# Layer 1's first channel-mixer product as seven products of halves for eight, past two blocks

## The chip, the cores and the metric

The kernel runs on one core of one Trainium2 chip. The metric is the device time of one execution in microseconds (us). Before the change it is 1830.53 us, the median of three runs (1828.48 to 1834.18).

## What is computed

Two layers of a diffusion backbone over 512 latent tokens (width 1024) and 256 context tokens. Each layer has a mixer (attention, retention and a state-space part over one input projection) and a channel mixer. In layer 1 the context's output is not needed, so its channel mixer works on 512 tokens alone. Cut to what matters here, all in float32:

```
h2 = rmsnorm(x, norm_g[2]) * (1 + sc2) + sh2            # 512 x 1024
u  = square(relu(h2 @ w_ff1))                           # w_ff1 1024 x 4096
x  = x + g2 * rmsnorm(u @ w_ff2, norm_g[3])             # w_ff2 4096 x 1024
```

## The kernel before, in words

Every float32 operand of a product is split into a rounded high part (ScalarE's copy to the `F32R` type) and a low part (the difference, taken by VectorE). A product is then three matmuls, high by high, high by low and low by high, which accumulate in one bank of PSUM. This is `mm3`, and it is why all matmuls of the profile have the lines L523, L524 and L525.

Weights come from HBM by DMAs on SP's queue, 512 KB at a time, into raw tiles (`wraw`, tag `wr`, three buffers). `wunit` splits them: ScalarE writes `wh` (L277), VectorE writes `wl` (L278). The pool `wp` has three buffers each of `wh` and `wl`, and every one holds 2048 columns, that is two raw tiles.

The channel mixer of layer 1 is `ff_phase(1, ...)`. It goes over eight blocks of 512 hidden columns. In a block:

- The first product, `ff1_part`, makes four banks `f`, each of 128 hidden columns by 512 tokens. A weight slice of 128 x 128 is the stationary operand, the tokens `h_h` and `h_l` move. A bank takes 8 x 3 matmuls of 512 columns, a block 96. For block 0, the four banks are begun earlier, in the output projection's stage, with 256 of the tokens; so its matmuls are 256 columns wide.
- The squared ReLU: ScalarE takes the ReLU out of PSUM (L1503), GpSimd squares (L1504), VectorE casts to `uh` (L1505) and subtracts to `ul` (L1506).
- The second product, `ff2`: for each of the four groups of 128 tokens (`tt`), two banks of 512 output columns in the PSUM tags `pb` and `pc` (two buffers each), 4 x 3 matmuls of 512 columns for each bank, 96 in a block. VectorE adds the banks to `acc` (L1532 copies in block 0, L1534 adds after it).

At the last block `sandwich` follows for each `tt`: the norm of `acc`, the gate, the residual and the store.

PSUM has eight banks: tag `pa` with two buffers of two banks, `pb` and `pc` with two of one bank each. The program's order is a priority: the framework builds each engine's own order when it compiles, from what is ready and which buffers are free, and each engine then runs that order.

## Time and profile before

| what | value |
|---|---|
| median of three runs | 1830.53 us (1828.48 to 1834.18) |
| profiled execution | 1831.16 us, span 1829.4 us |
| mean granted clock of TensorE | 0.979 |
| TensorE (PE) busy | 1737.7 us, 95% of the span |
| weight loads (PEld) busy | 1433.7 us, 78% |
| VectorE (DVE) busy | 1208.8 us, 66% |
| ScalarE (ACT) busy | 701.7 us, 38% |
| GpSimd (POOL) busy | 342.4 us, 19% |

The span runs from the first to the last instruction; the execution's own time is a little longer. A matmul's recorded duration overlaps the next one's, so the cost of one matmul in a stream is the distance from start to start, not its duration. The columns of the views are told beside their first rows below.

### The profile page before, as it was taken

How to read it: one execution, taken by the hardware profiler on the slowest of the kernel's cores; microseconds unless marked ns; L12 is line 12 of the kernel's file. 1: busy time of each engine (PE TensorE's matmuls, PEld its weight loads, DVE VectorE, ACT ScalarE, POOL GpSimd, SP SyncE). 2: the span in 40 equal slices, each digit the busy share in tenths (PEclk: the TensorE clock that was granted, in tenths of full speed). 3: DMA queues.
4: the chain of work that ended last, by engine and by line, in shares of the span. 5: the costliest groups of instructions: out<-in, count | busy, mean ns of one | idle time of the engine just before them, and what ended most of it. 6: DMA issues, size and time to landing. Idle time of an engine off the chain costs nothing. (4 is left out here: it accounts for less than half of the span.)

```text
span 1829.4 us, 24602 instructions
## 1 busy us (share of the span) xinstructions
PE 1737.7 (95%) x8991; PEld 1433.7 (78%) x8991; DVE 1208.8 (66%) x2474; ACT 701.7 (38%) x1270; POOL 342.4 (19%) x376
## 2 busy tenths in 40 slices
PE   7998999998999999999999999999988999999997
PEld 2887978657777888888888878887877788888886
DVE  5788976767567566566566587898877644444445
ACT  5553366743561201211201266545762622222222
POOL 0127222312000100100100111453121111111112
PEclk9999999998999999999999999999987999999999
DMA  8420443476435434444344443233343523333332
GB/s 282 123 61 30 133 123 101 119 204 177 162 120 137 126 105 126 128 113 117 116 116 116 128 150 116 68 106 104 106 121 85 179 67 94 102 94 100 104 95 92
DMA packets 189077, 217.00 MB, mean 119 GB/s; under 512 B 67666, under 2 KB 142236, under 8 KB 188956
## 3 DMA queue, kind: packets, MB, share of 16 engines
q1 hardware_dynamic: 188956, 215.43, 39.7%
q8 instruction: 71, 1.16, 0.3%
q14 instruction: 50, 0.41, 0.1%
HBM read 189.66 MB, written 25.72 MB: 118 GB/s over the span
## 5 line engine op out<-in xcount | busy, mean ns | idle before, releaser
L523 PE MATMUL f<-h_h,wh_f 128*128 128x512 f32 (+1 forms) x800 | 281.2, 352 | 1.4 <-ACT h_h L504 1.4
L524 PE MATMUL f<-h_l,wh_f 128*128 128x512 f32 (+1 forms) x800 | 281.7, 352 | 0.8 <-DVE h_l L505 0.8
L525 PE MATMUL f<-h_h,wl_f 128*128 128x512 f32 (+1 forms) x800 | 282.3, 353 | 0.0
L523 PE MATMUL f<-wh_g,uh 128*128 128x512 f32 x640 | 252.8, 396 | 4.6 <-DVE acc L1532 1.9
L524 PE MATMUL f<-wl_g,uh 128*128 128x512 f32 x640 | 252.5, 394 | 0.0
L525 PE MATMUL f<-wh_g,ul 128*128 128x512 f32 x640 | 251.8, 393 | 0.0
L1504 POOL TENSOR_TENSOR r<-r 128x768 f32<-128x768 f32 (+1 forms) x64 | 94.0, 1469 | 834.2 <-ACT r L1503 823.1
L277 ACT ACTIVATE wh_f<-wr_f 128x1024 fp32r<-128x1024 f32 x64 | 66.4, 1054 | 375.2 <-PE f L525 135.4
L1534 DVE TENSOR_TENSOR acc<-acc,f 128x512 f32<-128x512 f32 x140 | 96.1, 687 | 120.8 <-PE f L525 119.4
L523 PEld LDWEIGHTS f<-h_h,wh_f 128*128 128x128 f32 x800 | 153.2, 192 | 23.4 <-ACT h_h L504 1.5
L524 PEld LDWEIGHTS f<-h_l,wh_f 128*128 128x128 f32 x800 | 152.2, 190 | 23.0 <-DVE h_l L505 1.0
L525 PEld LDWEIGHTS f<-h_h,wl_f 128*128 128x128 f32 x800 | 152.4, 191 | 20.9
L461 DVE SCALAR_TENSOR_TENSOR ga<-wr_mg,cg_a,ga 128x512 f32<-128x512 f32 x216 | 153.7, 764 | 15.2 <-DMA wr_mg<-in_w_mod_dram 15.1
L523 PEld LDWEIGHTS f<-wh_g,uh 128*128 128x128 f32 x640 | 120.1, 188 | 33.9 <-DVE acc L1532 2.3
L525 PEld LDWEIGHTS f<-wh_g,ul 128*128 128x128 f32 x640 | 120.2, 188 | 28.6
L524 PEld LDWEIGHTS f<-wl_g,uh 128*128 128x128 f32 x640 | 120.3, 188 | 27.3
L1503 ACT ACTIVATE r<-f 128x768 f32<-128x768 f32 (+1 forms) x64 | 44.7, 698 | 192.2 <-PE f L525 128.2
L1505 DVE CAST uh<-r 128x768 fp32r<-128x768 f32 (+1 forms) x64 | 32.3, 505 | 123.7 <-POOL r L1504 123.7
L278 DVE TENSOR_TENSOR wl_g<-wr_g,wh_g 128x1024 fp32r<-128x1024 f32 x62 | 76.7, 1242 | 53.8 <-ACT wh_g L277 53.8
L278 DVE TENSOR_TENSOR wl_f<-wr_f,wh_f 128x1024 fp32r<-128x1024 f32 x64 | 77.7, 1221 | 50.1 <-ACT wh_f L277 50.1
L277 ACT ACTIVATE wh_g<-wr_g 128x1024 fp32r<-128x1024 f32 x64 | 67.3, 1056 | 96.6 <-DMA wr_g<-in_w_ff_dram 55.2
L523 PE MATMUL xbc<-h_h,wh_xbc 128*128 128x512 f32 (+1 forms) x208 | 71.9, 345 | 1.9 <-ACT cin L785 1.9
(403 smaller groups left out, 3711.0 us busy)
## 6 DMA issues: line engine op xcount, KB each, us to landing
wr_f<-in_w_ff_dram SPq DMA_DIRECT2D x64, 512.0 KB, 3.8
wr_g<-in_w_ff_dram SPq DMA_DIRECT2D x64, 512.0 KB, 3.6
wr_mg<-in_w_mod_dram SPq DMA_DIRECT2D x192, 128.0 KB, 2.9
wr_m<-in_w_mod_dram SPq DMA_DIRECT2D x24, 512.0 KB, 4.0
m<-in_w_mod_dram SPq DMA_DIRECT2D x32, 256.0 KB, 5.1
wr_o<-in_w_out_dram SPq DMA_DIRECT2D x16, 512.0 KB, 4.2
wr_xbc<-in_w_in_dram SPq DMA_DIRECT2D x14, 512.0 KB, 5.4
xmid<-xt SPq DMA_DIRECT2D x10, 512.0 KB
```

Of the source, the lines that this page charges most:

```text
L277: S.activation(hv[:, a0 : a0 + an], r, AF.Copy)
L278: (lo_eng or V).tensor_tensor(lv[:, a0 : a0 + an], r, hv[:, a0 : a0 + an].bitcast(F32), ALU.subtract)
L461: V.scalar_tensor_tensor(acc[:, s], r2[:, k % 2], w, acc[:, s], ALU.mult, ALU.add)
L523: T.matmul(o, a[0], b[0], start=first, stop=False)
L524: T.matmul(o, a[0], b[1], start=False, stop=False)
L525: return T.matmul(o, a[1], b[0], start=False, stop=last)
L1503: S.activation(r, q[:, :NT], AF.Relu)
L1504: G.tensor_tensor(r, r, r, ALU.mult)
L1505: V.tensor_copy(uh, r)
L1534: V.tensor_tensor(acc[tt][:, ns], acc[tt][:, ns], qs[tt][half], ALU.add)
```

## The change

From its third block on (3072 of 4096 hidden columns), the first product of layer 1's channel mixer is made by one level of Strassen's form. Tokens, inner dimension and hidden columns are each cut into two halves, and seven products of halves stand for eight; the combinations of halves are formed by additions. `ff_phase` gives way for layer 1 to a new function, `ff_seven`:

- Blocks 0 and 1 stay plain. Their squares move from GpSimd to ScalarE, and so does the cast to the high part.
- Six units `u` take the place of blocks 2 to 7. A unit has 256 hidden columns of the one half and 256 of the other. It loads four raw quarter tiles (512 KB each), GpSimd forms four sums of them (`weight_sum`), and `weight_part` splits seven operands. Each product has 2 x 4 x 3 matmuls of 256 columns.
- Once, GpSimd adds up the four quarters of the tokens and forms four differences (`tw`, `tx`); `token_part` splits them.
- Products are gathered outside PSUM: three sums in SBUF (`sums`), then four results `x` by VectorE; ReLU, square and cast by ScalarE.
- The second product keeps its matmuls, in two parts for each group of tokens (`s...0` and `s...1`). Its first weights lie in a buffer of their own.
- All steps are units with names, and a list (`PLAN[2]`) gives their order. `sandwich` takes its tiles from the tag `rw`.

The diff, cut:

```diff
+    RW=6,
+    UB=2,
+    XQ=2,
...
+    2: """
+        a010 a001 lw10 l200 a000 l201 tw12 a011 a100 wr012 s000 s001 s020 s021 wr022 lw11 s030 s031 s010 a110
+        s011 wr011 tw11 tw22 tx11 tx12 tx22 wr021 wp00 tw21 ws01 l210 ws03 a101 ws02 wr111 wp01 a111 p00 wr112
+        s110 wp02 tx21 l211 s111 tp1 s120 s100 wp03 s101 tp4 p01 tp2 wp04 s130 wp05 s121 tp3 p02 q00 q01 wr122
...
+        wr522 s501 q40 s521 q41 s530 ws44 wp46 q42 wr512 l261 q43 s511 s531 p50 ws51 s600 wp51 p51 ws52 wp52
+        s630 p52 wp54 s631 s620 s621 ws53 l270 wp53 s610 s601 q50 wp55 s611 q52 l271 q51 ws54 wp56 q53 s700
+        s701 s710 s711 s720 s721 s730 s731
+    """.split(),
...
-    def sandwich(pool, o, gate, xsrc, xdst, tt, nl, nwhich, hT, eng, bufs=2, half_bank=None, geng=None):
-
-        xt = pool.tile([128, D], F32, tag="xt", name="xt", bufs=bufs)
-        t = pool.tile([128, D], F32, tag="tt", name="tt", bufs=bufs)
+    def sandwich(pool, o, gate, xsrc, xdst, tt, nl, nwhich, hT, eng, bufs=2, half_bank=None, geng=None, tags=("xt", "tt")):
+
+        xt = pool.tile([128, D], F32, tag=tags[0], name="xt", bufs=bufs)
+        t = pool.tile([128, D], F32, tag=tags[1], name="tt", bufs=bufs)
...
+    def ff_seven(l, fp, h2T, pre):
+        NQ = 4
+        NS = 2
+        HID = (FF - NS * 512) // 2
+        acc = [fp.tile([128, D], F32, tag="acc", name=f"acc{l}{t}", bufs=NQ) for t in range(NQ)]
+        NB = FF // 512
+        w1, qpre = pre
+        hh, hl = h2T
+        rw = lambda name: fp.tile([128, 1024], F32, tag="rw", name=f"{name}{l}", bufs=KNOBS["RW"])
+        q4 = lambda ap: ap.rearrange("p (t k c) -> p t k c", t=2, k=4)
+        k4 = lambda ap: ap.rearrange("p (k c) -> p k c", k=4)
+        UNITS, AFTER = {}, {}
+        def unit(name, f, *after):
+            UNITS[name] = f
+            AFTER[name] = [n for n in after if n]
+        part = lambda ap, j, t: ap[:, 2 * t : 2 * t + 2, 4 * j : 4 * j + 4, :]
+        B = {"11": (0, 0), "12": (0, 1), "21": (1, 0), "22": (1, 1)}
+        side = {n: (part(hh, *B[n]), part(hl, *B[n])) for n in B}
+        full = {}
+        def whole(n):
+            b = q4(rw(f"b{n}"))
+            G.tensor_tensor(b, side[n][0].bitcast(F32), side[n][1].bitcast(F32), ALU.add)
+            full[n] = b
+        def token_part(n, b):
+            b = full[b]
+            dst = side["12"] if n == "t4" else tuple(q4(fp.tile([128, 1024], F32R, tag=f"{n}{i}", name=f"{n}{i}{l}")) for i in "hl")
+            S.activation(dst[0], b, AF.Copy)
+            V.tensor_tensor(dst[1], b, dst[0].bitcast(F32), ALU.subtract)
+            side[n] = dst
+        def sub(o, a, b):
+            G.tensor_tensor(full[o], full[a], full[b], ALU.subtract)
+        std = [f"a{NS - 1}{v}{fc}" for v in range(2) for fc in range(2)]
+        for n in ("12", "11", "22", "21"):
+            unit(f"tw{n}", lambda n=n: whole(n), "a000")
+        unit("tx11", lambda: sub("11", "12", "11"), "tw11", "tw12")
+        unit("tx12", lambda: sub("12", "22", "12"), "tw22", "tx11")
+        unit("tx22", lambda: sub("22", "22", "11"), "tx12")
+        unit("tx21", lambda: sub("21", "21", "22"), "tw21", "tx22")
+        unit("tp2", lambda: token_part("t2", "22"), "tx22")
+        unit("tp1", lambda: token_part("t1", "11"), "tx22")
+        unit("tp3", lambda: token_part("t3", "12"), "tx12")
+        unit("tp4", lambda: token_part("t4", "21"), "tx21", "tw12", *std)
+        raw, op, slot = {}, {}, {}
+        def weight_load(u, n):
+            i, j = int(n[0]) - 1, int(n[1]) - 1
+            raw[u, n] = k4(rw(f"w{n}_{u}"))
+            nc.sync.dma_start(raw[u, n], krows(w_ff1[l], 4 * j, 4, 512 * NS + 256 * u + HID * i, 256))
+        def weight_sum(u, o, a, b, how):
+            if (u, o) not in raw:
+                raw[u, o] = k4(rw(f"{o}_{u}"))
+            G.tensor_tensor(raw[u, o], raw[u, a], raw[u, b], how)
+        def weight_part(u, i, n):
+            if i % 2 == 0:
+                h, lo = (wp.tile([128, 2144], F32R, tag=t, name=f"{t}_s{l}{u}{i}", bufs=3) for t in ("wh", "wl"))
+                slot[u, i], slot[u, i + 1] = ((k4(h[:, o : o + 1024]), k4(lo[:, o : o + 1024])) for o in (0, 1024))
+            h, lo = slot[u, i]
+            S.activation(h, raw[u, n], AF.Copy)
+            V.tensor_tensor(lo, raw[u, n], h.bitcast(F32), ALU.subtract)
+            op[u, i] = h, lo
+        def product(q, a, n):
+            for c in range(2):
+                fs = slice(c * 128, (c + 1) * 128)
+                qv = q[:, c].rearrange("p (t c) -> p t c", c=128)
+                for k in range(4):
+                    mm3(qv, (a[0][:, k, fs], a[1][:, k, fs]), (side[n][0][:, :, k, :], side[n][1][:, :, k, :]),
+                        k == 0, k == 3)
+        def hidden(U, half, x):
+            ts = slice(256 * half, 256 * half + 256)
+            S.activation(x, x, AF.Square)
+            S.activation(U[0][:, :, ts], x, AF.Copy)
+            V.tensor_tensor(U[1][:, :, ts], x, U[0][:, :, ts].bitcast(F32), ALU.subtract)
+        Us = {}
+        def new_u(b, s):
+            if (b, s) not in Us:
+                Us[b, s] = tuple(fp.tile([128, 2, 512], F32R, tag=f"u{i}", name=f"u{i}{l}{b}{s}", bufs=KNOBS["UB"]) for i in "hl")
+            return Us[b, s]
+        xq = lambda name: fp.tile([128, 2, 256], F32, tag="xq", name=f"{name}{l}", bufs=KNOBS["XQ"])
+        pq = lambda name, i: fp.tile([128, 2, 256], F32, tag=f"pq{i}", name=f"{name}{l}")
+        ps, sums = {}, {}
+        def first(u, i):
+            if i == 0:
+                ps[u] = pA([128, 2, 2, 256], f"s0{l}{u}")
+                sums[u] = [pq(f"p{j}_{u}", j) for j in range(3)]
+                p1, u1, u4 = sums[u]
+                product(ps[u][:, 0], op[u, 0], "11")
+                S.activation(p1, ps[u][:, 0], AF.Copy)
+            elif i == 1:
+                p1, u1, u4 = sums[u]
+                product(ps[u][:, 1], op[u, 1], "t1")
+                V.tensor_tensor(u4, p1, ps[u][:, 1], ALU.add)
+            else:
+                p1, u1, u4 = sums[u]
+                A = pA([128, 2, 2, 256], f"s1{l}{u}")
+                product(A[:, 0], op[u, 2], "t2")
+                V.tensor_tensor(u1, p1, A[:, 0], ALU.add)
+                V.tensor_tensor(u4, u4, A[:, 0], ALU.add)
+        LATE = (("t3", 1, 1, 2, 3), ("t4", 1, 0, 1, 4), ("21", 0, 0, 0, 5), ("22", 0, 1, 2, 6))
+        def rest(u, i):
+            n, s, half, a, o = LATE[i]
+            q = (pB, pC)[i % 2]([128, 2, 256], f"s{i + 2}{l}{u}")
+            product(q, op[u, o], n)
+            if i == 0:
+                V.tensor_tensor(sums[u][1], sums[u][1], q, ALU.add)
+            x = xq(f"c{i}_{u}")
+            V.tensor_tensor(x, sums[u][a], q, ALU.add)
+            S.activation(x, x, AF.Relu)
+            hidden(new_u(u + NS, s), half, x)
+        def plain(b, v, fc):
+            w = w1[v] if b == 0 else wst[b, v]
+            q = qpre[2 * v + fc] if b == 0 else pA([128, TOK], f"f1{l}{b}{v}{fc}")
+            ff1_part(q, h2T, w, fc, 256 if b == 0 else 0, 512)
+            x = xq(f"r{b}{v}{fc}").rearrange("p a c -> p (a c)")
+            S.activation(x, q[:, 0:512], AF.Relu)
+            S.activation(x, x, AF.Square)
+            U = new_u(b, v)
+            S.activation(U[0][:, fc], x, AF.Copy)
+            V.tensor_tensor(U[1][:, fc], x, U[0][:, fc].bitcast(F32), ALU.subtract)
+        wst, w2, qs, gates = {}, {}, {}, []
...
+        def w2_load(b, v):
+            r0 = 4 * NS + 2 * (b - NS)
+            r = (4 * b + 2 * v) if b < NS else r0 + v * (HID // 128)
+            w2[b, v] = wunit(wcols(w_ff2[l], r, [(0, 0, 1024)]), (128, 2, 1024), f"g{l}{b}{v}", None, fp if v == 0 else None)
+        def second(b, tt, s):
+            cols = slice(tt * 128, (tt + 1) * 128)
+            if s == 0:
+                qs[b, tt] = [P([128, 512], f"f2{l}{b}{tt}{half}") for half, P in enumerate((pB, pC))]
+            U = Us[b, s]
+            for half in range(2):
+                ns = slice(half * 512, (half + 1) * 512)
+                q = qs[b, tt][half]
+                for i in range(2):
+                    mm3(q, (U[0][:, i, cols], U[1][:, i, cols]), (w2[b, s][0][:, i, ns], w2[b, s][1][:, i, ns]),
+                        s + i == 0, s + i == 2)
+                if s == 0:
+                    continue
+                if b == 0:
+                    V.tensor_copy(acc[tt][:, ns], q)
+                else:
+                    V.tensor_tensor(acc[tt][:, ns], acc[tt][:, ns], q, ALU.add)
+            if s and b == NB - 1:
+                if not gates:
+                    gates.append(gate_row(fp, l, 1, 0))
+                sandwich(fp, (acc[tt][:, 0:512], acc[tt][:, 512:1024]), gates[0], rows(xmid[l], tt), rows(out[0], tt),
+                         tt, l + 1, 0, None, G if tt < NQ - 1 else V, 6, None, G if tt < NQ - 1 else V, ("rw", "rw"))
...
+        for b in range(NB):
+            for v in range(2):
+                unit(f"l2{b}{v}", lambda b=b, v=v: w2_load(b, v))
+            u = b - NS
+            if u >= 0:
+                for n in ("11", "21", "22", "12"):
+                    unit(f"wr{u}{n}", lambda u=u, n=n: weight_load(u, n))
+                unit(f"ws{u}1", lambda u=u: weight_sum(u, "s1", "21", "22", ALU.add), f"wr{u}21", f"wr{u}22")
+                unit(f"ws{u}2", lambda u=u: weight_sum(u, "s2", "s1", "11", ALU.subtract), f"ws{u}1", f"wr{u}11")
+                unit(f"ws{u}3", lambda u=u: weight_sum(u, "21", "11", "21", ALU.subtract), f"ws{u}1")
+                unit(f"ws{u}4", lambda u=u: weight_sum(u, "12", "12", "s2", ALU.subtract), f"ws{u}2", f"wr{u}12", f"wp{u}5")
+                for i, (n, a) in enumerate((("11", "wr{}11"), ("s1", "ws{}1"), ("s2", "ws{}2"), ("21", "ws{}3"), ("22", "wr{}22"),
+                                            ("12", "wr{}12"), ("12", "ws{}4"))):
+                    unit(f"wp{u}{i}", lambda u=u, i=i, n=n: weight_part(u, i, n), a.format(u), f"wp{u}{i - 1}" if i % 2 else None)
+                for i, t in enumerate((None, "tp1", "tp2")):
+                    unit(f"p{u}{i}", lambda u=u, i=i: first(u, i), f"wp{u}{i}", t, f"p{u}{i - 1}" if i else None)
+                for i, t in enumerate(("tp3", "tp4", None, None)):
+                    unit(f"q{u}{i}", lambda u=u, i=i: rest(u, i), f"wp{u}{i + 3}", t, f"p{u}2", f"q{u}0" if i else None)
+            for tt in range(NQ):
+                for v in range(2):
+                    made = [f"a{b}{v}{fc}" for fc in range(2)] if u < 0 else [f"q{u}{i}" for i in ((2, 3), (0, 1))[v]]
+                    unit(f"s{b}{tt}{v}", lambda b=b, tt=tt, v=v: second(b, tt, v), f"l2{b}{v}", *made, f"s{b}{tt}0" if v else None,
+                         f"s{b - 1}{tt}1" if b else None)
...
-        ff_phase(1, fp, h2T, pre, None)
+        ff_seven(1, fp, h2T, pre)
```

## Rows read from the trace of the kernel before

**Rows 1.** Busy time by engine in a stretch: start:end, length, busy, counts, clock, DMA.

```profile
core 0: us, PE busy (x) PEld busy (x) DVE busy (x) ACT busy (x) POOL busy (x), PEclk, DMA share, GB/s
...
1486.00:1819.60 333.60, 333.60 (x1437) 270.06 (x1436) 146.58 (x193) 76.75 (x100) 49.66 (x35) 1.00 0.29 94
```

**Rows 2.** Timeline of PE, first product, 512 columns: start, duration, instruction.

```profile
1552.05 0.39 PE L523 MATMUL f<-h_h,wh_f 128*128 128x512 f32 x1
...
1570.07 0.39 PE L523 MATMUL f<-h_h,wh_f 128*128 128x512 f32 x1
```

**Rows 3.** Timeline of PE, second product, and its last matmul.

```profile
1803.87 0.40 PE L523 MATMUL f<-wh_g,uh 128*128 128x512 f32 x1
...
1819.27 0.40 PE L523 MATMUL f<-wh_g,uh 128*128 128x512 f32 x1
...
1819.73 0.40 PE L525 MATMUL f<-wh_g,ul 128*128 128x512 f32 x1
```

**Rows 4.** Timeline where block 0 ends: 256-column matmuls behind the first 512-column ones.

```profile
1480.10 0.39 PE L523 MATMUL f<-wh_g,uh 128*128 128x512 f32 x1
...
1481.41 1.25 DVE L1505 CAST uh<-r 128x512 fp32r<-128x512 f32 x1 [0.93 <-POOL r L1504]
...
1482.72 0.50 PE L523 MATMUL f<-wh_g,uh 128*128 128x512 f32 x1 [1.76 <-DVE uh L1505]
...
1483.29 0.28 PE L523 MATMUL f<-h_h,wh_f 128*128 128x256 f32 x1
...
1483.41 0.19 PEld L525 LDWEIGHTS f<-h_h,wl_f 128*128 128x128 f32 x1
...
1485.78 0.29 PE L523 MATMUL f<-h_h,wh_f 128*128 128x256 f32 x1
```

**Rows 5.** Groups of instructions, 1486.0 to 1819.6 us: count, busy us, mean ns, idle before.

```profile
L1504 POOL TENSOR_TENSOR r<-r 128x512 f32<-128x512 f32 x29 | 41.1, 1416 | 276.1 <-ACT r L1503 276.1
L1534 DVE TENSOR_TENSOR acc<-acc,f 128x512 f32<-128x512 f32 x54 | 37.1, 688 | 67.8 <-PE f L525 67.6
L278 DVE TENSOR_TENSOR wl_g<-wr_g,wh_g 128x1024 fp32r<-128x1024 f32 x28 | 34.2, 1223 | 34.0 <-ACT wh_g L277 34.0
L277 ACT ACTIVATE wh_g<-wr_g 128x1024 fp32r<-128x1024 f32 x28 | 29.5, 1055 | 53.6 <-PE f L524 32.8 <-DMA wr_g<-in_w_ff_dram 20.8
L1506 DVE TENSOR_TENSOR ul<-r,uh 128x512 fp32r<-128x512 f32 x29 | 20.0, 689 | 0.5
L1503 ACT ACTIVATE r<-f 128x512 f32<-128x512 f32 x29 | 17.1, 588 | 28.7 <-issue 23.5 <-PE f L525 5.1
L1505 DVE CAST uh<-r 128x512 fp32r<-128x512 f32 x29 | 12.4, 427 | 39.3 <-POOL r L1504 39.3
```

**Rows 6.** GpSimd's 128x1024 subtraction of weights: min/median/max ns, first and last start.

```profile
L278 POOL TENSOR_TENSOR wl_g<-wr_g,wh_g x2: 2394/2400/2407, 1454.2 to 1456.6; 128x1024 fp32r<-128x1024 f32 x2
```

**Rows 7.** Timelines of DVE and POOL where their instructions overlap, and one alone.

```profile
1564.20 1.22 DVE L278 TENSOR_TENSOR wl_g<-wr_g,wh_g 128x1024 fp32r<-128x1024 f32 x1 [3.02 <-ACT wh_g L277]
...
1564.73 1.59 POOL L1504 TENSOR_TENSOR r<-r 128x512 f32<-128x512 f32 x1 [4.73 <-ACT r L1503]
1569.61 1.04 POOL L1504 TENSOR_TENSOR r<-r 128x512 f32<-128x512 f32 x1 [3.29 <-ACT r L1503]
...
1815.04 3.52 POOL L1437 TENSOR_TENSOR tt<-acc,gr 128x512 f32<-128x512 f32 x2 [2.33 <-DVE acc L1534]
...
1817.60 0.97 DVE L1438 TENSOR_TENSOR oss<-oss 128x1 f32<-128x1 f32 x1 [0.85 <-ACT junk L1435]
...
1823.70 0.16 DVE L1438 TENSOR_TENSOR oss<-oss 128x1 f32<-128x1 f32 x1
```

**Rows 8.** The chain that ended last, from PE's end on: start, us, what.

```profile
1822.25 0.61 DVE acc L1534
...
1824.87 0.75 DVE xt L1441
1825.62 0.66 DVEq L1676
```

More of the change, by code (lines that the diff above doesn't have):

```diff
@@ L115 @@
         wo8
+    """.split(),
[3 more added lines that the diff above has]
+        s110 wp02 tx21 l211 s111 tp1 s120 s100 wp03 s101 tp4 p01 tp2 wp04 s130 wp05 s121 tp3 p02 q00 q01 wr122
+        wp10 s131 q02 wr121 ws11 ws04 wp06 p10 q03 wp11 ws13 p11 ws12 l220 wp12 wr221 l221 wp13 p12 s210 s200
+        s230 s231 wr222 wr211 s201 s220 wp14 s221 q10 ws21 wr212 wp15 ws14 ws22 wp20 q12 wp16 s211 ws23 wr322
+        wp22 q13 l230 q11 wp21 p20 s300 s310 p21 l231 p22 wp23 s320 wp24 wp25 s301 ws24 q20 wp26 s330 q23
+        wr311 s321 wr321 s311 wp30 q22 s331 ws31 ws32 p30 q21 l240 wp32 s400 wp31 ws33 p31 wp34 s410 wr312 p32
+        wr412 s430 wp33 l241 s401 s411 q30 wr411 s420 wr422 wp35 q32 q31 ws34 s431 s421 wp36 wr421 wp40 p40
+        l250 l260 ws41 wp41 wr511 l251 ws42 q33 s510 s500 wp42 p41 ws43 wp43 s520 wp44 wp45 wp50 wr521 p42
+        wr522 s501 q40 s521 q41 s530 ws44 wp46 q42 wr512 l261 q43 s511 s531 p50 ws51 s600 wp51 p51 ws52 wp52
+        s630 p52 wp54 s631 s620 s621 ws53 l270 wp53 s610 s601 q50 wp55 s611 q52 l271 q51 ws54 wp56 q53 s700
+        s701 s710 s711 s720 s721 s730 s731
     """.split(),
@@ L1551, in ff_phase, with w1_load @@
         return (hTn, kvw) if wc else None
+    def ff_seven(l, fp, h2T, pre):
[116 more added lines that the diff above has]
+        wst, w2, qs, gates = {}, {}, {}, []
+        def w1_load(b, v):
+            wst[b, v] = load_w1(l, b, v)
+        def w2_load(b, v):
[24 more added lines that the diff above has]
+                         tt, l + 1, 0, None, G if tt < NQ - 1 else V, 6, None, G if tt < NQ - 1 else V, ("rw", "rw"))
+        for b in range(NS):
+            for v in range(2):
+                if b:
+                    unit(f"lw{b}{v}", lambda b=b, v=v: w1_load(b, v))
+                for fc in range(2):
+                    unit(f"a{b}{v}{fc}", lambda b=b, v=v, fc=fc: plain(b, v, fc), f"lw{b}{v}" if b else None)
+        for b in range(NB):
[17 more added lines that the diff above has]
+            for tt in range(NQ):
+                for v in range(2):
+                    made = [f"a{b}{v}{fc}" for fc in range(2)] if u < 0 else [f"q{u}{i}" for i in ((2, 3), (0, 1))[v]]
+                    unit(f"s{b}{tt}{v}", lambda b=b, tt=tt, v=v: second(b, tt, v), f"l2{b}{v}", *made, f"s{b}{tt}0" if v else None,
+                         f"s{b - 1}{tt}1" if b else None)
+        plan = PLAN[2]
+        assert sorted(plan) == sorted(UNITS), set(plan) ^ set(UNITS)
+        seen = set()
+        for n in plan:
+            assert all(a in seen for a in AFTER[n]), (n, [a for a in AFTER[n] if a not in seen])
+            UNITS[n]()
+            seen.add(n)
```

## The prediction

> **What bounds the kernel now.** The share of busy time by engine comes first (the table above): PE 95%, no other compute engine over 66%. A mean over stages can mislead, so the stretches come next [rows 1]. [...] The waits agree: DVE stood 67.6 us until PE was done with a bank [rows 5], PE waited for nobody. So this stage lasts as long as its matmuls, and what counts is the distance between their starts.
>
> Three such prices are needed. First product, 512 columns: from 1552.05 to 1570.07 us there are 78 steps, 18.02/78 = 0.2310 us each [rows 2]. Second product: 66 steps in 15.40 us, 0.2333 us [rows 3]. 256 columns: 21 steps from 1483.29 to 1485.78 us, 2.49/21 = 0.1186 us [rows 4]; I use 0.119, the rounded value.
>
> Do they rebuild the stage? The second product starts at 1480.10 us [rows 4], the last matmul at 1819.73 us [rows 3], so with its own 0.23 us the stretch is 339.9 us. Seven blocks of 96 x (0.2310 + 0.2333) are 312.0, block 0's second product is 22.4, 24 matmuls of 256 columns still to come are 2.9, and one wait is 1.8 [rows 4]: 339.1. Only 0.8 us is unexplained; the prices hold.
>
> Behind PE stands a tail of 9.4 us up to 1829.4: the last additions to `acc`, the norm, the last residual at 1824.87 us, the stores [rows 8].
>
> **The change part by part.**
>
> Matmuls. A unit replaces 96 x 0.2310 = 22.18 us by 7 x 24 = 168 matmuls of 256 columns, 168 x 0.119 = 19.99 us. Six units give 6 x 2.19 = 13.1 us. An eighth of the 133.1 us in question would be 16.6 us; the rest goes because 0.119 is more than half of 0.2310. With 0.1186 the gain is 13.5 us. The second product keeps its 96 matmuls a block.
>
> Weight loads rise from 96 to 168 in a unit, and each is recorded with 0.19 us, longer than the 0.119 us between two starts [rows 4]. Those rows are such a stream already (one load before every 256-column matmul), and it runs at 0.119 us. So loads overlap and I add nothing.
>
> [...]
>
> ACT. Before, a block had 8 weight copies of 1.055 us and 4 ReLUs of 0.588 us, 10.8 us [rows 5]. A unit has 11 copies (7 for the products, 4 for `w_ff2`) and 13 passes over 128x512 (one copy of a product, then ReLU, square and cast four times). The trace has no pass of this sort from SBUF in the stretch; I take the ReLU's 0.588 us, and twice that as the upper bound. 11.6 + 7.6 = 19.2 us (26.9 at the bound) in a unit of 19.99 + 22.40 = 42.4 us. Covered by PE.
>
> DVE. Before: 8 x 1.223 + 4 x (0.427 + 0.689) + 8 x 0.688 = 19.8 us [rows 5]. A unit: 11 subtractions of weights, 13.5; 8 additions of products out of PSUM, 5.5; 4 subtractions of `u`, 2.8; 8 additions to `acc`, 5.5; together 27.2 us, 64% of 42.4. Covered, if it comes in time.
>
> POOL. Before: four squares of 1.416 us, 5.7 us a block. A unit has four `weight_sum` of 128x1024 with two inputs, 2.40 us each by the nearest row [rows 6], 9.6 us. Once, 8 more for the tokens, 19.2 us, while blocks 0 and 1 give PE 22.4 + 2.9 + 44.6 = 69.9 us of work.
>
> DMAs. 8 loads of 512 KB a unit on SP's queue, as in a block before, no byte more. A load now waits for one of six `rw` buffers instead of three `wr`; only `w_ff2` still uses the latter.
>
> What is new is how tightly these depend on each other. Three places can let PE wait:
>
> *The port between DVE and POOL.* A POOL square alone took 1.04 us; one that began while DVE subtracted weights (1564.20 to 1565.42) took 1.59 and ended 0.90 us after DVE was done. The other way round, an addition of 128x1, 0.16 us elsewhere, took 0.97 us and ended at 1818.57, 0.01 us after POOL's pair (1815.04 + 3.52) [rows 7]. So an instruction of one engine stands until the other's is over. [...] DVE can so be held for up to 2.40 us, four times a unit, and behind it in DVE's queue stand the additions that free PSUM and the `u` that PE needs next. The cover is PE's own rhythm: a product lasts 24 x 0.119 = 2.86 us, half of a token group's second product 12 x 0.2333 = 2.80 us. One delay just fits under one such piece; two in a row do not.
>
> *The banks.* `pb` and `pc` now serve both the second product and the last four products of a unit. A piece can start only when one of two banks of its tag has been emptied, 0.69 to 1.38 us of DVE's time after a piece of 2.8 us.
>
> *The weights' buffers.* Five fills of three `wh`/`wl` pairs a unit, with 1.06 + 1.22 us after each release. And the last operand hangs on a chain: split of `12`, 2.40 us on POOL, split again.
>
> The trace of before shows none of these stalls, so I bound them: below, nothing (PE did wait for nobody for 333.6 us); above, all 24 sums at 2.40 us, 57.6 us. I take 0.7 us a unit, 4.2 us: near the lower end, since every wait has a piece of PE's work about its own length before it.
>
> The start. The 1.8 us wait of 1482.72 us came from a cast on DVE that took 1.25 instead of 0.43 us [rows 4, 5]; the cast moves to ACT, and the list puts 24 matmuls of block 1 (5.5 us) before the second product. It may vanish or find a successor: -1.0, between -1.8 and 0.
>
> The tail keeps its operations: DVE's last addition now comes a shorter piece after its neighbour (6 matmuls instead of 12), within 1 us either way; 0.
>
> **Sum** against the profiled execution: 1831.2 - 13.1 - 1.0 + 4.2 = 1821.3 us. The median of the runs is 0.6 us lower, so 1820.7; I say 1820.5 us, 0.55% faster. About 0.3%, 5.5 us, is what a measurement of this kernel can tell from no change.
>
> **Rivals.**
>
> *Given back in the stage, chance 0.20.* The banks and buffers above cost 1.4 to 3.2 us a unit, that is 8.5 to 19 us; in the middle, 2.2 us a unit or 13 us, the time is 1831.2 - 13.1 - 1.0 + 13 = 1830.1. For it: five fills of three buffers, and chains through POOL. Against: no engine is over 64% busy, and PE stood still nowhere in the stretch before.
>
> *Slower by the port, 0.12.* Place: DVE's queue behind `weight_sum`. If every sum holds DVE so that PE loses 1.25 of its 2.40 us, that is 24 x 1.25 = 30 us: 1831.2 - 13.1 - 1.0 + 30 = 1847. It decides from 14.1/24 = 0.59 us a sum on. For it: the rows of mutual waiting. Against: squares of 1.42 us met the same subtractions 29 times [rows 5] and PE saw nothing.
>
> *The weight load is the bound, 0.04.* Should loads of 0.188 us not overlap, a unit's products take 168 x 0.188 = 31.6 us, 9.4 us more than before, 56 us over six units: 1887. [...] Only rows of another kind of stream could bear this out; those shown deny it.
>
> **Chances and range.** The forecast holds 0.64. Faster by over 0.3% (below 1825): 0.65, with a part of the first rival's edge; within 0.3%: 0.20; slower: 0.15. The likeliest case alone spans 1814 (no stall, the better price, no start wait, 1 us off the tail: 1831.2 - 13.5 - 1.8 - 1.0, less 0.6 for the median) to 1825. For 8 in 10 the range must take in most of the first rival: 1814 to 1832.
>
> **What would show it.** In the new trace: 256-column matmuls 0.119 us apart in the units; distance from the second product's first matmul to the last that shrinks by about 13 us less the stalls; PE's idle time in the units 0 to 1 us each, named by DVE's additions or by POOL's sums. If start distances are above 0.125 us, the price was wrong. If PE idles more than 2 us a unit, the row that releases it says which place it was: a bank (an addition on DVE), a weight's part (DVE or ACT behind `rw`), or DVE rows stretched from 1.22 to 2 us and more beside POOL. Wrong it would be above all if several such waits meet in every unit.

## The result and the profile after

The changed kernel takes 1814.68 us (median of 4 runs, 1813.68 to 1818.94) against 1830.7 us, a ratio of 0.990 with a 95% interval of 0.9884 to 0.9917: faster by 1.0% (by the two medians 16.0 us, 0.9%). The forecast was 1820.5 us, 0.55%. The profiled execution took 1814.29 us, its span is 1812.5 us, 16.9 less than before. (Compare execution with execution: 1831.16 to 1814.29.)

First the busy time by engine over the span, then the stretch that answers to [rows 1]: start:end, length, then busy time and count for each engine, granted clock, DMA share.

```profile
PE 1727.0 (95%) x9423; PEld 1446.6 (80%) x9423; DVE 1269.9 (70%) x2514; ACT 765.3 (42%) x1362; POOL 380.2 (21%) x374
```

```profile
core 0: us, PE busy (x) PEld busy (x) DVE busy (x) ACT busy (x) POOL busy (x), PEclk, DMA share, GB/s
...
1486.80:1804.40 317.60, 315.33 (x1847) 276.32 (x1846) 200.53 (x236) 131.57 (x180) 77.78 (x33) 1.00 0.29 93
```

PE is still the bound: idle for 2.27 us of 317.60, all of it one wait at the start. DVE's busy share rose from 44% to 63% of the stretch, ACT from 23% to 41%, POOL from 15% to 24%. The view of waits says which waits PE had from 1440 us to the end:

```profile
engine line waited for: us in total, times, longest us
PE f L542 <- DVE ul L1716: 2.3, 1, 2.3
PE nps L225 <- ACT tt L527: 1.9, 1, 1.9
PE f L541 <- DVE h_l L522: 0.8, 1, 0.8
PE f L540 <- ACT h_h L521: 0.6, 1, 0.6
```

None of these lies in the six units. Line 1716 is a subtraction for `u` in blocks 0 and 1; the other three stand ahead of the second product. Now the timeline of PE in a unit: the first and a later matmul of 256 columns (answers to [rows 4]), 63 steps apart.

```profile
1564.42 0.28 PE L540 MATMUL s<-h_h,wh_s 128*128 128x256 f32 x1
...
1571.92 0.28 PE L540 MATMUL s<-h_h,wh_s 128*128 128x256 f32 x1
```

7.50/63 = 0.119 us, as in the stream that was there before; the mean over 979 such steps in all units is 0.1188. The groups of instructions of the same stretch give the other engines' prices: count, busy us, mean ns, idle before.

```profile
L295 DVE TENSOR_TENSOR wl_g<-wr_g,wh_g 128x1024 fp32r<-128x1024 f32 x29 | 43.5, 1524 | 10.2 <-ACT wh_g L294 10.1
L1644 DVE TENSOR_TENSOR wl_s<-w,wh_s 128x1024 fp32r<-128x1024 f32 x30 | 38.4, 1292 | 5.8 <-ACT wh_s L1643 5.7
...
L1636 POOL TENSOR_TENSOR s<-w,w 128x1024 f32<-128x1024 f32 x6 | 17.4, 2906 | 25.3 <-DVE wl_s L1644 24.9 <-POOL w L1636 0.2
...
L1659 ACT ACTIVATE c<-c 128x512 f32<-128x512 f32 x24 | 15.0, 625 | 0.4
```

A pass of ACT takes 0.625 us (0.588 assumed), a sum on POOL 2.91 in the costliest of four groups and 2.47 in the cheapest (2.40 assumed), the subtractions of `w_ff2` 1.52 instead of 1.22 on DVE [rows 5]: POOL and DVE do hold each other up, and PE does not see it.

**Where the 16.9 us came from.** I measure from the first 256-column matmul of the first product (1452.91 before, 1454.90 us after), since the work ahead of it is the same. From there to the end of the span it was 376.49 and is 357.60 us, 18.9 less; 2.0 were lost ahead of it, and that start moved between 1447.9 and 1461.7 us over the profiles of this study without any change to that work.

| from that matmul on | before | after | difference |
|---|---|---|---|
| matmuls of six units: 6 x 96 x 0.2319, 6 x 168 x 0.1188 | 133.6 | 119.7 | -13.8 |
| second product, 768 matmuls, mean step 0.2332 and 0.2309 | 179.1 | 177.3 | -1.8 |
| gaps and slow steps ahead of the second product | 6.4 | 2.4 | -4.0 |
| wait near its start (PE, step in excess) | 1.9 | 2.4 | +0.5 |
| PE's steps above the mean, from there on | 0.1 | 1.8 | +1.7 |
| from PE's end to the end of the span | 9.4 | 7.8 | -1.6 |

Together -19.0, against 18.9 measured. The means are over all steps of a kind in the timeline, gaps and slow steps taken out. The 6.4 us are a gap of 3.4, 0.8 in eight slow transposes (0.106 us a step elsewhere) and 2.2 us of slow matmuls; the 2.4 are two gaps of 0.8 and 0.9 and 0.7 us of slow steps.

**Ahead of the second product.** Before, the timelines of POOL, DVE and PE show this (start, duration, instruction, and in brackets the idle time before it with what ended it; the last row is a window of busy times, as above):

```profile
1454.22 4.75 POOL L278 TENSOR_TENSOR wl_g<-wr_g,wh_g 128x1024 fp32r<-128x1024 f32 x2 [43.03 <-ACT wh_g L277]
...
1455.28 1.36 DVE L233 SCALAR_TENSOR_TENSOR rm_t<-ors,rm_h 128x1 f32<-128x1 f32 x1
1456.68 2.31 DVE L237 SCALAR_TENSOR_TENSOR ors<-rm_t,ors 128x1 f32<-128x1 f32 x1
...
1465.45 1.97 PE L208 MATMUL nps<-ident,tt 128*128 128x128 f32 x8 [3.26 <-ACT tt L510]
...
1468.08 0.41 PE L525 MATMUL f<-h_h,wl_f 128*128 128x256 f32 x1
1468.29 0.41 PE L523 MATMUL f<-h_h,wh_f 128*128 128x256 f32 x1
...
1466.50:1472.50 6.00, 6.00 (x36) 6.00 (x35) 2.60 (x5) 2.56 (x5) 0.00 (x0) 0.62 0.01 4
```

POOL split block 0's first `w_ff2` weights just then, and two DVE instructions on 128x1, 0.22 and 0.16 us elsewhere, took 1.36 and 2.31. They belong to a norm of a token group; the next group's norm came late behind them, and PE stood for 3.26 us. After that, matmuls of 256 columns start 0.21 us apart instead of 0.12, and the last row gives a granted clock of 0.62 from 1466.5 to 1472.5 us (it was 1.00 from 1452.9 to 1462.0 us, before the wait). For the eight transposes right behind the wait it was 0.50 (1465.4 to 1467.1 us). After the change:

```profile
1458.28 0.21 DVE L250 SCALAR_TENSOR_TENSOR rm_t<-ors,rm_h 128x1 f32<-128x1 f32 x1
...
1459.54 0.15 DVE L254 SCALAR_TENSOR_TENSOR ors<-rm_t,ors 128x1 f32<-128x1 f32 x1
...
1464.40 1.09 PE L225 MATMUL nps<-ident,tt 128*128 128x128 f32 x8
...
1466.50:1472.50 6.00, 4.63 (x37) 4.22 (x36) 3.19 (x3) 3.66 (x5) 2.84 (x2) 1.00 0.29 84
```

No wait over 0.3 us stands before these transposes, and the clock is 1.00 in the same window. The new function splits these weights on DVE, and into a buffer of their own.

**Near the start of the second product** six of the token sums run on POOL without a break, and DVE's two-input instructions stretch beside them, up to the one PE waits for. Timelines of POOL, DVE and PE after (answers to the wait in [rows 4]):

```profile
1469.66 9.08 POOL L1599 TENSOR_TENSOR b<-h_h,h_l 128x1024 f32<-128x1024 f32 x3 [56.50 <-DVE h_l L522]
1478.70 9.02 POOL L1610 TENSOR_TENSOR b<-b,b 128x1024 f32<-128x1024 f32 x3
...
1470.57 5.92 DVE L295 TENSOR_TENSOR wl_g<-wr_g,wh_g 128x1024 fp32r<-128x1024 f32 x2 [1.13 <-ACT wh_g L294]
1476.42 5.70 DVE L1716 TENSOR_TENSOR ul<-r,uh 128x512 fp32r<-128x512 f32 x2
1482.05 6.75 DVE L295 TENSOR_TENSOR wl_g<-wr_g,wh_g 128x1024 fp32r<-128x1024 f32 x2
1488.72 0.68 DVE L1716 TENSOR_TENSOR ul<-r,uh 128x512 fp32r<-128x512 f32 x1
...
1489.46 0.50 PE L542 MATMUL f<-wh_g,ul 128*128 128x512 f32 x1 [2.27 <-DVE ul L1716]
```

Three pairs on DVE take 18.37 us where 2 x 1.22 + 2 x 0.69 + 2 x 1.22 = 6.3 would do.

**The second product** runs at two paces. A piece, half of a token group's share of a block, is 12 matmuls. These are the first matmuls of three pieces in a row (timeline after); the first piece reads the weights in the buffer of their own, the second those in a shared one:

```profile
1494.66 0.39 PE L540 MATMUL f<-wh_g,uh 128*128 128x512 f32 x1
...
1497.39 0.40 PE L540 MATMUL f<-wh_g,uh 128*128 128x512 f32 x1
...
1500.18 0.39 PE L540 MATMUL f<-wh_g,uh 128*128 128x512 f32 x1
```

2.73/12 = 0.2275 us with the weights from the buffer of their own, 2.79/12 = 0.2325 with those from the shared one; before, all took 0.2333 [rows 3].

**Behind PE**, DVE (timeline, answers to [rows 8]) begins its last addition at 1805.23, 0.56 us after PE's end at 1804.67; before it was 2.3 us.

```profile
1803.90 0.68 DVE L1745 TENSOR_TENSOR acc<-acc,f 128x512 f32<-128x512 f32 x1
...
1805.23 0.68 DVE L1745 TENSOR_TENSOR acc<-acc,f 128x512 f32<-128x512 f32 x1
```

### The profile page after: what moved, and what is told of

It reads as the page before. It is cut to its first block, busy times and chain, and to the rows that moved or that the text cites. A ratio compares the mean times of both kernels' runs of the same rounds, so it can differ in the third digit from the quotient of the medians.

```text
span 1812.5 us, 25628 instructions
## 1 busy us (share of the span) xinstructions
PE 1727.0 (95%) x9423; PEld 1446.6 (80%) x9423; DVE 1269.9 (70%) x2514; ACT 765.3 (42%) x1362; POOL 380.2 (21%) x374
## 4 chain that ended last, share of the span: by engine, by line
PE 57%; DVE 9%; DMA 3%; ACT 3%; issue 2%; POOL 1%; SPq 0%; DVEq 0%; POOLq 0%; ACTq 0%
PE f L540 12%; PE f L542 12%; PE f L541 12%; PE s L540 2%; PE s L541 2%; PE s L542 2%; PE op L540 2%; PE op L541 2%; PE op L542 2%; DVE wl_g L295 1%; DMA wr_mg<-in_w_mod_dram 1%; PE pv L1139 1%; DVE ga L478 1%; DVE acc L812 1%; PE nps L225 1%
## 5 line engine op out<-in xcount | busy, mean ns | idle before, releaser
L540 PE MATMUL f<-h_h,wh_f 128*128 128x256 f32 (+1 forms) x608 | 205.9, 339 | 2.0 <-ACT h_h L521 2.0
L541 PE MATMUL f<-h_l,wh_f 128*128 128x256 f32 (+1 forms) x608 | 205.0, 337 | 1.5 <-DVE h_l L522 1.5
L542 PE MATMUL f<-h_h,wl_f 128*128 128x256 f32 (+1 forms) x608 | 205.3, 338 | 0.0
L1521 POOL TENSOR_TENSOR r<-r 128x768 f32<-128x768 f32 x32 | 49.6, 1550 | 537.7 <-ACT r L1520 527.0
L540 PEld LDWEIGHTS f<-h_h,wh_f 128*128 128x128 f32 x608 | 115.7, 191 | 15.4 <-ACT h_h L521 2.3
L541 PEld LDWEIGHTS f<-h_l,wh_f 128*128 128x128 f32 x608 | 115.6, 190 | 15.3 <-DVE h_l L522 1.9
L542 PEld LDWEIGHTS f<-h_h,wl_f 128*128 128x128 f32 x608 | 115.6, 190 | 13.0
L1551 DVE TENSOR_TENSOR acc<-acc,f 128x512 f32<-128x512 f32 x84 | 57.5, 685 | 54.1 <-PE f L542 52.9
L1520 ACT ACTIVATE r<-f 128x768 f32<-128x768 f32 x32 | 25.9, 808 | 160.3 <-PE f L542 124.2
L542 PE MATMUL xbc<-h_h,wl_xbc 128*128 128x512 f32 (+1 forms) x208 | 71.4, 343 | 0.0
```

What stands on the lines that cost most here:

```text
L540: T.matmul(o, a[0], b[0], start=first, stop=False)
L541: T.matmul(o, a[0], b[1], start=False, stop=False)
L542: return T.matmul(o, a[1], b[0], start=False, stop=last)
L1520: S.activation(r, q[:, :NT], AF.Relu)
L1521: G.tensor_tensor(r, r, r, ALU.mult)
L1551: V.tensor_tensor(acc[tt][:, ns], acc[tt][:, ns], qs[tt][half], ALU.add)
```

## The experiments

Theory: the gain is the products of halves, some 13 us, with almost nothing given back in the units; the rest (4 us ahead of the second product, 2 us of its pace) comes from side effects of two small edits. Rivals: the new order and engines of the whole stage bring the gain, or the units do lose time where DVE and POOL hold each other up (what the prediction calls the port) and something else makes up for it. The "stretch" in the table is the time from that first matmul to the end of the span, in the one profile of each run.

| run | median us | ratio to before (95%) | stretch us |
|---|---|---|---|
| before | 1830.7 to 1834.4 by group of runs | 1 | 376.49 |
| after | 1814.68 | 0.990 (0.9884 to 0.9917) | 357.60 |
| after_again | 1817.64 | 0.9907 (0.9882 to 0.9931) | 359.14 |
| a_plain | 1830.41 | 0.9993 (0.9978 to 1.0008) | 371.79 |
| a_split_g | 1817.53 | 0.9926 (0.9902 to 0.9950) | 359.33 |
| b_split_v | 1830.28 | 0.9986 (0.9971 to 1.0002) | 372.54 |
| b_w2_own | 1833.2 | 0.9999 (0.9984 to 1.0014) | 375.23 |
| a_tok_v | 1815.73 | 0.9897 (0.9878 to 0.9916) | 356.20 |
| a_sum_twice | 1832.14 | 0.9991 (0.9978 to 1.0005) | 373.57 |
| a_shift32 | 1815.48 | 0.9894 (0.9876 to 0.9912) | 356.67 |
| a_sum_v | 1816.9 | 0.9906 (0.9886 to 0.9926) | 357.56 |
| b_split_shift | 1826.41 | 0.9958 (0.9942 to 0.9973) | 371.14 |
| a_tok_shift | 1810.41 | 0.9871 (0.9852 to 0.9889) | 354.30 |
| a_all_v | 1807.27 | 0.9857 (0.9836 to 0.9879) | 354.26 |

**The new function without products of halves (a_plain).** All eight blocks plain, in an order of their own; no token sums, no sums of weights.

```diff
-        NS = 2
+        NS = 8
...
-        plan = PLAN[2]
+        plan = []
+        for b in range(NB):
...
+            plan += [f"a{b}00", f"a{b}01"]
...
```

> The changed kernel with all eight blocks plain (eight products instead of seven in every block, no sums of tokens or weights), in the same form of listed units, with a list of my own in the order of the blocks. Theory: what the products of halves save is 6 x (96 x 0.2319 - 168 x 0.1188) = 13.8 us, and the stalls that they bring are below 1.5 us; so this kernel takes 12 to 14 us more than the changed one, 1827 to 1829 us, and stays 2 to 4 us below before. Rival: the restructured stage is worth most of the 16 us, and the products little; then this kernel stays below 1820 us.

In the time, the stage as such is worth nothing that could be measured: the interval goes from 4.0 us faster to 1.5 us slower. (The stretch of its one profile is 4.7 us shorter than before.) Beside a_split_g, timed on the same chip, the products of halves bring 1830.41 - 1817.53 = 12.9 us; in the profiles from the first matmul to PE's end it is 362.57 - 349.77 = 12.8 against the changed kernel. The rival of the new order falls, as the one cause of the gain. That 12.8 lies so near the table's 13.8 is in part luck: a_plain loses 3.1 us more than the changed kernel ahead of the second product, behind a wait of its own for `h_h`, but has no wait at its start and fewer slow steps behind it (4.1 us together).

**Block 0's split back on POOL (a_split_g)**, in the changed kernel:

```diff
-   w2[b, v] = wunit(..., f"g{l}{b}{v}", None, fp if v == 0 else None)
+   w2[b, v] = wunit(..., f"g{l}{b}{v}", G if b == 0 and v == 0 else None, fp if v == 0 else None)
```

> The changed kernel, with block 0's first half of w_ff2 split by GpSimd again, as before the change. Theory: a stall of 3 to 4 us comes back ahead of the stage, VectorE rows of 0.2 us stretch to over 1 us beside the GpSimd ones, and the time rises by 3 to 5 us to about 1818.5 us. Rival: the time is that of the changed kernel, 1814.7 us, as the order of the queues is another now.

The stall did not come back; what I expected failed. POOL's timeline says why:

```profile
1466.34 2.41 POOL L1599 TENSOR_TENSOR b<-h_h,h_l 128x1024 f32<-128x1024 f32 x1 [56.50 <-DVE h_l L522]
1468.70 4.75 POOL L295 TENSOR_TENSOR wl_g<-wr_g,wh_g 128x1024 fp32r<-128x1024 f32 x2
```

The split now begins behind the last `h_l`, past the norms, whose DVE rows (1454.94 and 1456.21 us) keep 0.21 and 0.15 us. So in the changed kernel it is not the engine that takes the split out of their way, but that the split begins later. The buffer is enough for that: in b_w2_own (below), where nothing but the buffer differs from before, POOL's split begins 17.5 us after the first matmul of the stretch, instead of 1.3. The time of 1817.53 us came near the 1818.5 expected without the cause expected: after_again, the unedited changed kernel, took 1817.64.

**The split off POOL in the kernel before (b_split_v).** The reverse test.

```diff
-  ..., f"g{l}{b}{v}", G if b == 0 and l in (1,) and v == 0 else None)
+  ..., f"g{l}{b}{v}", None)
```

> The kernel before, with one word of the change: the low part of block 0's first half of w_ff2 is made by VectorE instead of GpSimd. Theory: in the trace of before two GpSimd subtractions of 2.40 us (1454.2 to 1459.0 us) hold VectorE, where a 0.16 us instruction takes 2.31 us; the norm of the last token group comes late, PE stands for 3.5 us and then runs 16 matmuls at the half clock. Without them this stretch (192 matmuls of 256 columns, 30.1 us) takes about 26 us as in the changed kernel, and the kernel is 3 to 5 us (0.2%) faster. Rival: the difference between the two profiles there is the scatter of one execution; then the stretch stays near 30 us in this profile and the time is that of before.

The 3.4 us gap is gone and the stretch 4.0 us shorter, as expected. In the time it is 2.6 us (0.14%), and the interval just includes no change.

**The buffer of their own in the kernel before (b_w2_own).**

```diff
-  ..., G if b == 0 and l in (1,) and v == 0 else None)
+  ..., G if b == 0 and l in (1,) and v == 0 else None, fp if l == 1 and v == 0 else None)
```

> The kernel before, with layer 1's first half of each block's w_ff2 in a buffer of its own in the stage's pool, as the change has it. Theory: the place of the moving operand sets the pace; the matmuls that read it run at 0.2277 us instead of 0.2333, those of the second half stay at 0.233, and the stage gets 2 us (0.1%) shorter. Rival: the pace in the changed kernel comes from the new shape of the u tiles or from the new work on DVE and POOL; then all stay at 0.233 us and the time is that of before.

The pace came: 0.2310 us in the mean instead of 0.2332, 1.7 us, and the stretch is 1.3 us shorter. The time does not show so little: its interval reaches from 2.9 us faster to 2.6 us slower. That the later split saved nothing more has a cause: in place of the gap behind POOL there are two of 2.4 and 1.0 us, with 3.1 us of slow steps, together 6.5 us where before had 6.4. Timelines of POOL, ACT and PE:

```profile
1476.38 4.70 POOL L278 TENSOR_TENSOR wl_g<-wr_g,wh_g 128x1024 fp32r<-128x1024 f32 x2 [59.23 <-ACT wh_g L277]
...
1471.70 1.07 ACT L277 ACTIVATE wh_g<-wr_g 128x1024 fp32r<-128x1024 f32 x1
1472.64 1.07 ACT L504 ACTIVATE h_h<-tt 128x1024 fp32r<-128x1024 f32 x1
...
1473.76 0.79 PE L523 MATMUL f<-h_h,wh_f 128*128 128x256 f32 x2 [2.24 <-ACT h_h L504]
```

A weight copy stands ahead of `h_h` in ACT's queue and delays it by about 1 us; PE's wait is 1.6 us longer than in the changed kernel (0.62), where the other 0.6 comes from I did not follow. In the changed kernel ACT goes from the transposes straight to `h_h`, so there the two side effects add.

**Token sums on DVE (a_tok_v)**, in the changed kernel:

```diff
-            G.tensor_tensor(b, side[n][0].bitcast(F32), side[n][1].bitcast(F32), ALU.add)
+            V.tensor_tensor(b, side[n][0].bitcast(F32), side[n][1].bitcast(F32), ALU.add)
...
-            G.tensor_tensor(full[o], full[a], full[b], ALU.subtract)
+            V.tensor_tensor(full[o], full[a], full[b], ALU.subtract)
```

> The changed kernel, with the eight sums and differences of the tokens on VectorE instead of GpSimd. Theory: in the changed kernel six of them stand on GpSimd back to back from 1469.7 to 1487.7 us, VectorE's instructions with two inputs from SBUF alternate with them and take 2.9 us instead of 0.7 to 1.2, and PE's wait of 2.27 us at 1489.46 comes from there. With VectorE alone these rows are back at 0.7 and 1.2 us, the wait goes, and the kernel is about 2 us faster than the changed one. Rival: VectorE, with 9.8 us more work in these 20 us, is late by itself; the wait stays at 2 us or grows.

The 2.27 us wait is gone. The stretch is only 1.4 us shorter, since in this profile 1.3 us more were lost ahead of the second product, where the granted clock was 0.50 from 1459.2 to 1462.4 us. The time is 1.9 us below after_again, with intervals that overlap. Eight more operations on DVE cost PE less than POOL's eight beside it, since the neighbours are back at their own length (timeline of DVE; a token sum takes 1.22 us here):

```profile
1486.22 1.22 DVE L1610 TENSOR_TENSOR b<-b,b 128x1024 f32<-128x1024 f32 x1
1487.36 1.22 DVE L295 TENSOR_TENSOR wl_g<-wr_g,wh_g 128x1024 fp32r<-128x1024 f32 x1
1488.49 0.68 DVE L1716 TENSOR_TENSOR ul<-r,uh 128x512 fp32r<-128x512 f32 x1
```

**Each sum of weights twice (a_sum_twice)**: POOL first forms each of the 24 sums into a tile that nobody reads.

```diff
+            G.tensor_tensor(k4(fp.tile([128, 1024], F32, tag="dbl", ...)), raw[u, a], raw[u, b], how)
             G.tensor_tensor(raw[u, o], raw[u, a], raw[u, b], how)
```

> The changed kernel, with each of the 24 sums of weights formed twice on GpSimd, the first time into a tile that nobody reads. Doubles the time in which GpSimd can hold VectorE in the units, from 4 to 8 instructions of 2.4 us in 42.4 us. Theory: a piece of PE's work of 2.8 us covers each delay, so the time rises by 0 to 3 us. Rival (the port as I feared it): each sum costs PE 0.59 us or more, 24 more cost 14 us or more.

I was wrong: it costs 14.5 us (1832.14 - 1817.64), the whole gain. Two of the nine new gaps, from the timelines of ACT and PE, and two groups of DVE:

```profile
1574.42 1.06 ACT L1644 ACTIVATE wh_s<-s 128x1024 fp32r<-128x1024 f32 x1 [7.69 <-POOL s L1637]
...
1580.88 0.58 PE L540 MATMUL s<-h_h,wh_s 128*128 128x256 f32 x1 [3.78 <-ACT wh_s L1644]
1583.10 0.58 PE L542 MATMUL s<-h_h,wl_s 128*128 128x256 f32 x1 [1.43 <-DVE wl_s L1645]
```

```profile
L295 DVE TENSOR_TENSOR wl_g<-wr_g,wh_g 128x1024 fp32r<-128x1024 f32 x31 | 59.8, 1953 | 10.1 <-ACT wh_g L294 10.0
L1645 DVE TENSOR_TENSOR wl_s<-w,wh_s 128x1024 fp32r<-128x1024 f32 x30 | 45.0, 1512 | 4.5 <-ACT wh_s L1644 4.5
```

At the largest gap ACT had stood for 7.69 us until POOL had formed `s`, and the operand that PE waits for came behind it in ACT's queue; most other gaps go back to DVE's weight splits and additions to `acc`, with the splits stretched beside POOL. The run does not part these two. It does show that the slack is limited: four sums a unit fit, eight don't.

**Sums of weights on DVE (a_sum_v)**: `G` becomes `V` in `weight_sum`.

> The changed kernel with the 24 sums of weights on DVE, the token sums still on POOL. Theory: the units change by under 1.5 us, as POOL's four sums a unit were covered; the start wait of 2.3 us stays, because the token sums cause it. Rival A (the port costs the units): 3 us or more faster. Rival B (DVE late): 5 us or more slower.

The stretch is 357.56 against 357.60 us: POOL's 24 sums cost PE nothing, and nothing is won by giving them to DVE. The start wait stays (2.25 us). Yet on POOL the sums did hold DVE up: without them there, the view of this tile gives, for DVE's weight splits, min/median/max ns of

```profile
L1644 DVE TENSOR_TENSOR wl_s<-w,wh_s x30: 1215/1220/1227, 1524.1 to 1783.9; 128x1024 fp32r<-128x1024 f32 x30
```

and with the sums on POOL (a_tok_v) the same line goes up to 2.4 us:

```profile
L1644 DVE TENSOR_TENSOR wl_s<-w,wh_s x30: 1209/1219/2381, 1520.9 to 1780.7; 128x1024 fp32r<-128x1024 f32 x30
```

**Everything on the left side of SBUF 32 bytes later (a_shift32).** In the built program the buffer of their own and the `u` tiles lie 32 bytes off a multiple of 64, the shared weight buffers on one. Does that offset set the pace, or the region of SBUF?

```diff
-    sel = cp.tile([128, 4], F32, name="sel")
+    sel = cp.tile([128, 12], F32, name="sel")
+    sel = sel[:, 0:4]
```

> The changed kernel, with one tile of the constants' pool 32 bytes longer, so that all tiles of the left side of SBUF, the shared weights' buffers and the tokens among them, begin 32 bytes later; nothing else differs. In the changed kernel, the u tiles and the own buffer of w_ff2 begin 32 bytes past a multiple of 64, the shared buffers at a multiple of 64; the pairs of the first kind run at 0.2277 us, those of the second at 0.2330. Theory: the alignment sets the pace; then all matmuls of the second product run at 0.228 us and the stage is 2 us shorter. Rival: it is the region of SBUF in which the buffers lie; then the paces stay, and so does the time.

With the shared buffers moved, the pieces that read them speed up too, in their old region. Timeline of PE, a piece from the shared buffer, 12 steps:

```profile
1497.13 0.39 PE L541 MATMUL f<-wh_g,uh 128*128 128x512 f32 x1
...
1499.86 0.39 PE L541 MATMUL f<-wh_g,uh 128*128 128x512 f32 x1
```

2.73/12 = 0.2275 us; the mean over the second product is 0.2291 instead of 0.2309. The first product, whose weights and tokens both move, stays at 0.2326 us. The stretch is 0.9 us shorter, the time 2.2 below after_again, again with intervals that overlap. So the offset counts, but how it combines with that of the other operand is open.

**The side effects alone (b_split_shift)**: the kernel before with b_split_v's and a_shift32's edits.

> The kernel before, without one product of halves, with the two side effects alone: block 0's first w_ff2 split kept off POOL, and the left side of SBUF 32 bytes later. Theory (side effects are terms of their own): the begin stretch 4 us shorter as in the run with the split alone, and 700 matmuls of the second product at 0.229 instead of 0.2333 us, 3 us; first matmul of the begin stretch to the span's end 376.5 in the kernel before, here 369 to 371; the time 5 to 7 us below the kernel before. Rival (they are no terms of their own: with PE paced otherwise another stall appears): 0 to 3 us below.

Faster by 0.42%, 7.7 us by the ratio; 5.4 in the stretch, a little under the 5.5 to 7.5 expected, since the mean step came to 0.2304 and not 0.229, though all weights and `u` tiles of that product lie 32 bytes off there. The profile does not show where the other 2.3 us come from: in it the stretch begins 4.2 us later than before. The rival's 0 to 3 us are excluded by the interval (5 to 11 us), so the side effects are terms of their own.

**After_again** is the changed kernel once more, on the chip of a_tok_v, a_sum_twice and a_shift32.

> The changed kernel once more, as the measure for the runs beside it on the same chip. Theory: a profile like the first one (1 us of stalls in the six units, a wait of 2.3 us where the second product begins, a tail of 7.8 us), time 15 to 18 us below before.

The time is as expected. The wait near the start of the second product is the same 2.27 us, but behind it the granted clock fell: 0.52 from 1489.0 to 1492.4 us, where the first profile kept 1.00. Eight matmuls of 512 columns started 0.43 us apart instead of 0.23, 1.6 us, which is all of the difference between the two stretches (359.14 and 357.60). In a_split_g the clock fell behind this wait as well (0.57 from 1487.0 to 1490.6 us). So single stretches that differ by some 1.5 us can differ by the clock alone, and in after_again, where it fell, the wait cost 3.9 us (2.27 + 1.6).

**The two edits together (a_tok_shift), and these with the sums on DVE too (a_all_v).**

> The changed kernel with both helpful edits at once: the eight token sums on DVE and everything on the left side of SBUF 32 bytes later. If the start wait (POOL's token sums holding DVE) and the pace of the second product are two separate terms, the gains add: first matmul of the begin stretch to the end of the span 357.6 us in the changed kernel, here 354 to 356, the start wait of 2.3 us gone and the second product at 0.229 us; the time 2 to 4 us below the changed kernel. Rival (scatter): the two earlier gains of about 2 us each were chance; then this run lies within 1 us of the changed kernel's 1815 to 1818.

> As the run with both helpful edits, and the 24 sums of weights on DVE too, so that POOL does nothing beside DVE in the units. Theory (the units' few short stalls are not the port's, DVE at 70% has room): 24 x 1.2 us more on DVE, but its rows beside POOL shrink by as much; within 1.5 us of the run with both edits, two-input rows at 1.22 instead of 1.3 to 1.5 us. Rival A (the port still costs the units): 2 us or more faster. Rival B (DVE becomes the late one): 5 us or more slower, PE's waits in the units released by DVE.

Both add to the change: the stretch is 354.3 us, 3.3 below the changed kernel, as expected. In the time, the interval of a_tok_shift still touches that of the changed kernel; that of a_all_v does not. In a_all_v the stretch is the same to 0.04 us, and PE waits nowhere from 1480 to 1795 us. Its time is 3.1 us lower all the same, in the profile all of it ahead of the stretch (1447.94 against 1452.70 us), where the two kernels do the same work; the intervals overlap. I count the two as equal. At 1807.27 and 1810.41 us they beat both kernels.

## Why the prediction missed

**The step that failed.** The sum had 4.2 us of stalls in the units, where 1.7 came, and it put two edits of the diff at nothing without a reason, which were worth 4.0 and 1.8 us. The time of 1814.68 us stands at the lower edge of the range, and that is luck: the edge of 1814 was reckoned without a start wait, which came, and without these two edits.

**Right in mechanism.** PE stayed the bound, a unit's 168 matmuls run at 0.119 us, loads overlap, the engines behind are covered. Six units make 1008 such matmuls, each with its own load of 0.19 us, and they ran 0.1188 us apart. None of the rivals happened. One reading was too strong: of the 29 squares of [rows 5], 21 met a subtraction of weights in the trace of before, not all; the others ran alone in 1.04 us.

**Matmuls, -13.1 forecast, -13.8 measured.** The window of [rows 2] gave 0.2310 for the first product; over all its steps it is 0.2319. The rest is the rounding of 0.1186 to 0.119.

**Stalls in the units, +4.2 forecast, +1.7 measured.** This is the largest mis-sized term of the sum. I had put 0.7 us on every unit for banks, buffers and the delays between DVE and POOL; in the profile no step of PE from 1490 us on is more than 0.12 us over its mean, and eighteen steps of about 0.1 us over it make up the 1.7. The argument that each wait has a piece of PE's work of its own length before it was right and should have been carried to its end. It has a limit: with eight sums a unit, 14.5 us of stalls appear. Per added sum that is 0.6 us, the second rival's deciding price of 0.59, reached only with twice its work.

**The start, -1.0 forecast, +0.5 measured.** The cast's wait vanished and found a successor, but one that I had not named: I let the token sums pass as "19.2 us, while PE has work" and did not ask which DVE instruction runs beside them. a_tok_v shows them as the cause. Here three pairs on DVE took 18.4 us instead of 6.3, and POOL's sums 3.0 instead of 2.4. But not every instruction of one engine stands until the other's is over, as I had it: in the timeline of the changed kernel from 1490 to 1804 us, six weight splits on DVE that began while POOL formed a sum took 2.13 to 3.12 us instead of 1.22, and 22 additions out of PSUM that began so kept their 0.67 to 0.69. The port was my name for what lies behind this; the runs show the times alone.

**The tail, 0 forecast, -1.6 measured.** DVE's last addition began 0.56 us behind PE instead of 2.3. a_plain, with the new function but whole blocks in another order, still has 9.2 us from PE's end, so the pieces of the second product alone don't do it; which part of the list does was not tried.

**What the sum lacked.** Two edits that I had read and not costed: block 0's `w_ff2` split leaving POOL's queue while the norms run (-4.0 us, as in b_split_v), and the buffer of their own (-1.8). The first is the largest miss of all. The first could be read from the trace before: [rows 6] are those very instructions, and I used them only as a price for another step. "Ahead of the second product" was outside the stretch that I looked at, though the diff changes what is issued there.

The sum gave 1821.3 us for the profiled execution, which took 1814.3: 7.0 us. The work ahead of the second product makes 4.0 of it, the stalls in the units 2.5, the pace 1.8, the tail 1.6, the matmuls 0.7, less 1.5 for the start and 2.0 lost ahead of the stretch: 7.1.

## What to carry to other kernels

Go through the diff by instruction, not by intent: a weight split that changes its engine or its buffer moves what stands beside it in time, so look at the rows next to its old place and its new one. Off the critical path, count a delay only where it is longer than the piece of work that covers it; four sums of 2.5 to 2.9 us on GpSimd cost nothing behind pieces of 2.8 us, eight cost the whole gain. And two small moves, token sums to VectorE and buffers 32 bytes on, were worth another 3 us of the stretch.
